# Who issues the last store, where GpSimd drains, and who clears the semaphores, at the end of a windowed attention kernel

## Chip, cores and metric

One core of a Trainium2 chip. The metric is the device time of one execution in microseconds (us), lower is better.

## The reference

```python
def reference(q, k, v):                      # each (4, 4096, 1536) float32
    W, scale = 64, 1536 ** -0.5
    # q, k, v cut into windows of 64 rows
    logits = einsum('bnwd,bnud->bnwu', q_w, k_w) * scale
    attn = softmax(logits)                   # within the window
    return einsum('bnwu,bnud->bnwd', attn, v_w)   # (4, 4096, 1536) float32
```

## The kernel before

The 16,384 rows are handled in N = 32 units of 512 rows. GpSimd issues nearly all transfers: loads of q, k, v with a cast to fp16 two units ahead, and one store of 3 MB per unit, by its software queue. SyncE starts the first loads and otherwise only watches landings. TensorE, VectorE and ScalarE compute. Only the end matters here: the last unit's store is split into two halves, so that the first can start before the last evictions are done.

```python
for u in range(1, N):                       # GpSimd's loop
    hand_over("q", u, q16, m_q, g_q)        # wait for the landing, copy, request the next load
    hand_over("k", u, k16, m_k, g_k)
    gp.wait_ge(m_q, u + 1)
    store(u - 1)                            # 3 MB, software queue, semaphore d_o[(u - 1) % 3]
    hand_over("v", u, v16, m_v, g_v)

base, o = (N - 1) * UR, outs[(N - 1) % NO]
for h, (eng, c) in enumerate(((gp, 1), (sy, 3))):   # first half GpSimd, second half SyncE
    for a in range(2):
        eng.wait_ge(n_e[a], c)              # evictions of VectorE and of ScalarE
    eng.dma_start(
        out=rows(of, base + R * P * h, R, R), in_=slots(o, R * h, R * h + R, R)
    ).then_inc(d_l[h], 16)
gp.drain()                                  # line 380
for i in range(NO):
    last = max(u for u in range(N - 1) if u % NO == i)
    sy.wait_ge(d_o[i], 16 * (last // NO + 1))
for i in range(2):
    sy.wait_ge(d_l[i], 16)                  # line 385
sy.sem_inc(done, 1)
gp.wait_ge(done, 1)
# ... lo, hi: the range of the kernel's semaphores
gp.sem_clear(range(lo, hi + 1))             # line 390
```

The softmax here doesn't subtract the row's maximum and nothing guards it: scores larger than these inputs give would overflow.

## Time and profile before

| | before |
|---|---|
| time, first three runs | 945.38 us (944.78 to 945.55) |
| the execution that was traced | 942.61 us, span 940.8 |
| 16 DMA engines | busy 90% or more in 39 of 40 slices |
| read and written | 402.65 MB, 428 GB/s over the span |
| GpSimd's drain | 928.4 to 939.6 |
| last landing | 939.04 |

For the tail, read the records of single source lines: the line, the engine (POOLq and SPq are the sequencers of GpSimd and SyncE), the operation, its duration in ns as minimum/median/maximum, and the first and last start in us of the span. A transfer's record holds its issue only; "DMA to landing" is the time from issue to the last count of its semaphore. The lines themselves stand in the prediction below.

### The profile page before, as it was taken

What the parts mean: (1) busy time and instruction counts of PE and PEld (TensorE: products, weight loads), DVE (VectorE), ACT (ScalarE), POOL (GpSimd) and SP (SyncE); (2) the same over time, 40 slices, a digit from 0 to 9 for tenths busy, and PEclk for the clock granted to TensorE, in tenths of its full rate; (3) what the DMA queues carried; (4) which work ended last, traced back from release to release, by engine and by line L of the source; (5) the groups of instructions that cost most, each with busy time, mean ns of one, the idle gap of its engine ahead of it and who ended that gap; (6) DMA issues with size and microseconds to landing.
All of it is one profiled execution on the core that took longest, in us unless ns stands there. A gap on an engine that the chain in (4) does not pass through costs nothing. (4 is left out here: it accounts for less than half of the span.)

```text
span 940.8 us, 11422 instructions
## 1 busy us (share of the span) xinstructions
PE 659.4 (70%) x4096; PEld 396.2 (42%) x3456; DVE 280.2 (30%) x453; ACT 335.6 (36%) x642; POOL 340.9 (36%) x229
## 2 busy tenths in 40 slices
PE   1888686766767767767677686776767767667673
PEld 1555244533444334454344443345534454334440
DVE  0443321333313333223332233322333223332232
ACT  1444333333333233332433333333333333343331
POOL 4344333344333442333423334333343333433221
PEclk9999978888888798877887978888888888797886
DMA  9999999999999999999999999999999999999998
GB/s 251 216 218 281 256 246 281 282 281 265 237 281 282 282 274 233 276 282 282 279 234 270 282 282 282 238 263 281 282 282 247 255 282 281 281 256 247 281 298 366
DMA packets 27084, 253.35 MB, mean 269 GB/s; under 512 B 2112, under 2 KB 2112, under 8 KB 10688
## 3 DMA queue, kind: packets, MB, share of 16 engines
q0 software_dynamic: 26352, 248.52, 100.4%
q1 hardware_dynamic: 720, 4.72, 1.3%
q14 instruction: 10, 0.08, 0.0%
q8 instruction: 2, 0.03, 0.0%
HBM read 301.99 MB, written 100.66 MB: 428 GB/s over the span
## 5 line engine op out<-in xcount | busy, mean ns | idle before, releaser
L157 PE MATMUL lt<-xq,xk 128*128 128x256 f16 x1536 | 215.5, 292 | 0.0
L145 PE MATMUL tp<-ident,k 128*128 128x128 f32 x768 | 148.5, 337 | 83.4 <-PEq L211 73.4
L294 POOL COPY v<-vl 128x3072 f32<-128x3072 f32 x31 | 85.2, 2747 | 295.9 <-DMA vl<-in_v_dram 295.9
L157 PEld LDWEIGHTS lt<-xq,xk 128*128 128x128 f16 x1536 | 159.8, 104 | 33.0
L145 PE MATMUL tp<-ident,q 128*128 128x128 f32 x768 | 110.8, 291 | 69.0 <-DVE xq L220 36.5
L145 PEld LDWEIGHTS tp<-ident,k 128*128 128x128 f32 x768 | 114.7, 175 | 103.3 <-issue 100.8
L186 PEld LDWEIGHTS <-et 128*128 128x128 f16 x384 | 35.0, 109 | 285.8 <-issue 280.3
L220 ACT COPY xk<-tp 128x512 f32<-128x512 f32 x96 | 59.3, 618 | 262.1 <-ACTq L211 262.1
L145 PEld LDWEIGHTS tp<-ident,q 128*128 128x128 f32 x768 | 90.1, 149 | 109.1 <-issue 108.4
L220 DVE COPY xk<-tp 128x512 f32<-128x512 f32 x96 | 66.5, 692 | 227.5 <-DVEq L211 227.5
L294 POOL COPY q<-ql 128x3072 f32<-128x3072 f32 x31 | 85.0, 2742 | 110.3 <-DMA ql<-in_q_dram 110.3
L294 POOL COPY k<-kl 128x3072 f32<-128x3072 f32 x31 | 85.2, 2747 | 106.9 <-DMA kl<-in_k_dram 106.9
L113 PE MATMUL o<-v,et 128*128 128x512 f16 x384 | 116.2, 448 | 0.0
L113 PE MATMUL sp<-ones,et 128*128 128x1 f16 x256 | 25.8, 170 | 116.6 <-PEq L211 114.3
L262 ACT ACTIVATE et<-lt,zeros 32x128 f16<-32x128 f32 x256 | 91.8, 359 | 39.4 <-ACTq L211 36.2
L220 ACT COPY xq<-tp 128x512 f32<-128x512 f32 x96 | 59.8, 623 | 121.3 <-ACTq L211 121.3
L249 DVE TENSOR_SCALAR out<-o,rs 128x512 f32<-128x512 f32 x128 | 91.3, 747 | 35.7 <-DVEq L211 31.7
L273 ACT ACTIVATE out<-tp,rs 128x512 f32<-128x512 f32 x64 | 44.0, 687 | 141.1 <-ACTq L211 110.9
L113 PE MATMUL tp<-v,et 128*128 128x512 f16 x256 | 92.8, 450 | 0.0
L220 DVE COPY xq<-tp 128x512 f32<-128x512 f32 x96 | 66.2, 690 | 88.7 <-DVEq L211 88.3
L239 DVE RECIPROCAL rs<-sp 128x2 f32<-128x2 f32 x64 | 10.7, 168 | 265.7 <-DVEq L211 265.2
L113 PE MATMUL lt<-v,et 128*128 128x512 f16 x128 | 58.2, 455 | 0.0
(22 smaller groups left out, 224.4 us busy)
## 6 DMA issues: line engine op xcount, KB each, us to landing
out_dram<-out POOLq DMA_DIRECT2D x31, 3072.0 KB, 61.8
ql<-in_q_dram POOLq DMA_DIRECT2D x31, 1536.0 KB, 54.9
kl<-in_k_dram POOLq DMA_DIRECT2D x31, 1536.0 KB, 54.9
vl<-in_v_dram POOLq DMA_DIRECT2D x31, 1536.0 KB, 54.9
out<-in_q_dram SPq DMA_DIRECT2D x1, 1536.0 KB, 13.4
k<-in_k_dram POOLq DMA_DIRECT2D x1, 1536.0 KB, 12.8
v<-in_v_dram POOLq DMA_DIRECT2D x1, 1536.0 KB, 19.4
out_dram<-out POOLq DMA_DIRECT2D x1, 1536.0 KB, 8.8
```

Of the source, the lines that this page charges most:

```text
L113: return nc.tensor.add_instruction(mybir.InstMatmult(name=nc.get_next_instruction_name(), engine=PE, ins=[low(rhs), low(w)], outs=[low(o)] ...
L145: ins = nc.tensor.transpose(tps[g % 2][:, r, j, :], pairs[:, c * P : (c + 1) * P], ident[:, :])
L157: ins = nc.tensor.matmul(lts[h][:, r, :, :], lhsT=halves(xk, c)[:, r, h, :, w], rhs=halves(xq, c)[:, :, h, :, w], start=(c == 0 and w == 0 ...
L186: ld = nc.tensor.ldweights(w)
L220: copy(out=dst, in_=tps[g % 2][:, :, :, :]).then_inc(f_c[g % 4], 1)
L239: ve.reciprocal(out=rs[:, n : n + R], in_=sp[:, n : n + R]).then_inc(n_d, 1)
L249: ins = ve.tensor_scalar_mul(scaled(u, n, j), bank(n, j), scalar1=rs[:, n : n + 1])
L262: ins = sc.activation(ets[h][s, :, :, s], lts[h][s, :, :, s], EXP, bias=zeros[s, 0:1], scale=scale)
L273: ins = sc.activation(scaled(u, n, j), bank(n, j), COPY, bias=0.0, scale=rs[:, n : n + 1])
L294: gp.tensor_copy(out=dst[:, :, :].bitcast(FP32), in_=landing[x][u % NL][:, :, :].bitcast(FP32)).then_inc(c_l, 1)
```

## The change

Three things at the very end of the program. Both halves are issued by SyncE. GpSimd's drain thereby stands behind the store of unit 30, the last one that GpSimd still issues, and GpSimd signals `done` when it is through. SyncE waits for `done` and the landings and clears the semaphores itself. The intent is to take GpSimd's issue, its drain and the hand-shake back to it out of the end of the chain.

```diff
-        for h, (eng, c) in enumerate(((gp, 1), (sy, 3))):
+        for h, c in enumerate((1, 3)):
             for a in range(2):
-                eng.wait_ge(n_e[a], c)
-            eng.dma_start(
+                sy.wait_ge(n_e[a], c)
+            sy.dma_start(
                 out=rows(of, base + R * P * h, R, R), in_=slots(o, R * h, R * h + R, R)
             ).then_inc(d_l[h], 16)
         gp.drain()
+        gp.sem_inc(done, 1)
+        sy.wait_ge(done, 1)
         # ... the waits for d_o and d_l on SyncE as before
-        sy.sem_inc(done, 1)
-        gp.wait_ge(done, 1)
-        gp.sem_clear(range(lo, hi + 1))
+        sy.sem_clear(range(lo, hi + 1))
```

## The prediction

> **What bounds the kernel now.** I read the page first, its slices above all, then the groups of DMA issues, the records of each source line of the tail, and last a table of stretches over the final 12 us. The two kernels differ only in the tail, so the question has two parts: what the whole run is bound by, and which event is the last one that somebody waits for.
>
> ```profile
> span 940.8 us, 11422 instructions
> ...
> DMA  9999999999999999999999999999999999999998
> ...
> q0 software_dynamic: 26352, 248.52, 100.4%
> q1 hardware_dynamic: 720, 4.72, 1.3%
> ...
> HBM read 301.99 MB, written 100.66 MB: 428 GB/s over the span
> ```
>
> The DMA row has nine tenths or more in 39 slices of 40; no compute engine is above 70%. The sum read and written, 402.65 MB, at the 428 GB/s shown is the span itself. Nothing in the change touches the 31 earlier stores or any load, so what can change is at most the last slice, 23.5 us of 940.8. A change of 2% would need 19 us, nearly all of that slice.
>
> Now the tail. Here are the issues of the last store (line 377, one half on each queue), GpSimd's drain (380), SyncE's waits for the landings (385), and GpSimd's clear (390), each with its duration in ns and its start:
>
> ```profile
> L377 POOL DMA_DIRECT2D out_dram<-out x1: 547/547/547, 928.4 to 928.4; - x1
> L377 SPq DMA_DIRECT2D out_dram<-out x1: 347/347/347, 929.5 to 929.5; - x1
> ...
> DMA to landing us min/median/max: 8.8/9.2/9.5
> ...
> L380 POOLq DRAIN  x1: 11193/11193/11193, 928.4 to 928.4; - x1
> ...
> L385 SPq EVENT_SEMAPHORE  x2: 17/22/28, 937.2 to 939.1; - x2
> ...
> L390 POOLq EVENT_SEMAPHORE_RANGE_CLEAR  x1: 353/353/353, 939.6 to 939.6; - x1
> ```
>
> The first half lands at 928.4 + 8.8 = 937.2, the second at 929.5 + 9.5 = 939.0, and SyncE passes its last wait at 939.1. It then signals `done`. But the clear on GpSimd starts only at 939.6: GpSimd's drain began at 928.4 and lasted 11.19 us, so it ended at 939.6. **The clear was held up by the drain, not by the landing.** That costs about 0.5 us at the end of the chain, and it is what the change removes. (The page's own chain of waits stops at 928.77 with VectorE, so it doesn't reach this tail; I read it from the line records.)
>
> Between them, the stretches (the six numbers in the middle are busy times of engines; DMA share and GB/s stand last):
>
> ```profile
> 929.00:930.00 1.00, 0.00 (x0) 0.00 (x0) 0.51 (x1) 0.00 (x0) 0.00 (x0) 1.00 0.99 418
> ...
> 932.00:934.00 2.00, 0.00 (x0) 0.00 (x0) 0.00 (x0) 0.00 (x0) 0.00 (x0) 0.67 1.03 434
> ...
> 936.00:937.00 1.00, 0.00 (x0) 0.00 (x0) 0.00 (x0) 0.00 (x0) 0.00 (x0) 0.50 0.96 406
> 937.00:938.00 1.00, 0.00 (x0) 0.00 (x0) 0.00 (x0) 0.00 (x0) 0.00 (x0) 0.50 0.43 184
> 938.00:939.00 1.00, 0.00 (x0) 0.00 (x0) 0.00 (x0) 0.00 (x0) 0.00 (x0) 0.50 0.12 49
> 939.00:940.00 1.00, 0.00 (x0) 0.00 (x0) 0.00 (x0) 0.00 (x0) 0.00 (x0) 0.50 0.00 0
> ```
>
> The 16 DMA engines are full from before 929 until about 937, and then drop out one by one until 938.7. When the last store is issued they still work on the store of unit 30 (issued 905.9); its 16 partial landings in the trace are spread from 929.6 to 931.7, so some DMA engines run 2.1 us behind the others. Each then has 8 + 8 packets of 12 KB of the last store, at a median of 460 ns each in the packet records: 16 x 0.46 = 7.4 us. The latest engine: 931.7 + 7.4 = 939.1, and the measured last landing is 939.04. So the latest DMA engine never ran dry, and **the landing of the last byte is set by the backlog of that engine, not by when or by whom the halves are issued.**
>
> **What the Trainium skill says.** "DMA: Bandwidth & Descriptors", section "Issuing engines are not separate DMA queues": transfers started by scalar, sync or gpsimd run on the same 16 DMA engines and interleave, and using several issuers saves only sequencer time. The trace agrees: both queues' packets take a median of 460 ns. The same page, "Latency and other measured facts", gives first bytes at about 0.6 us for the hardware path and 1 us for the software one. At the kernel's start, SyncE's first load was issued at 0.96 and its first packet ran at 1.97, so 1.0 us here; the advantage of some tenths is open. "Perfetto Trace Analysis", section "Sequencer-only Instruction (DRAIN, etc)", says that a record holds the execution and not the wait for semaphores. That agrees with the clear (353 ns, its wait for `done` not in it), and it says how to read the drain: it carries no semaphore, so its 11.19 us are its own execution, waiting for the DMAs. I found no statement on what a drain of GpSimd waits for.
>
> **The change part by part.**
> 1. First half from SyncE in place of GpSimd. The issue moves from 928.40 to about 927.9 (SyncE's condition, the third and fourth evictions of the last unit, is met at 927.88 by the semaphore records; GpSimd took 0.5 us more). The issue costs 0.35 in place of 0.55 us. Gain on the end: zero, as the latest DMA engine is busy until 931.4 with earlier work. In the traces' DMA share a dip of 0.1 for half a microsecond at 929.3 should vanish; it is on early engines, with slack of nearly 2 us.
> 2. Second half. SyncE is free of the first issue by 928.3 and still waits for VectorE's last output (its record ends at 929.51). The issue stays at 929.5. Zero.
> 3. The drain moves ahead: it now stands behind the issue of unit 30's store and the last copy of v (917.15 + 2.74 = 919.9). In the kernel before, it ended 2.3 us after the last landing on GpSimd's own queue (939.57 - 937.23). Unit 30's store lands at 931.7, or up to about 934.5 if the six or so packets still due on the latest engine alternate with packets of the first half (6 x 0.46 = 2.8 us). Plus 2.3 gives 934 to 937, ahead of 939.0: off the path. Removed from the path: 939.57 - 939.13, SyncE's last event to the end of the drain, about 0.45 us.
> 4. The clear moves to SyncE, right behind its last wait: start 939.1 in place of 939.6. I take the same 0.353 us, as it is a sequencer's work on the same range of semaphores. But before, SyncE went through its end-of-section hand-shake (four events of about 0.07 us, line 302, 939.2 to 939.4) beside GpSimd's drain and clear; now that stands behind the clear. So not all of 0.45 is gained. Working along SyncE: clear 939.10 to 939.45, first event 939.50, last gather 939.73, its no-op 939.79, its drain of the exit barrier 939.85. Before, that drain began at 940.11. Net: **-0.26 us**.
> 5. The exit barrier from there (940.11 to 940.83) is the same: 0.
>
> Sum: 0 + 0 - 0.45 + 0.19 = -0.26 us, 0.03% of the time. 945.38 - 0.26 = 945.1 us.
>
> **The rivals.**
> (a) *The drain waits for every DMA of the core, not for GpSimd's own.* Then it still ends half a microsecond behind the last landing, `done` comes at 939.6, and SyncE's clear follows: end at about the old place, 945.3 to 945.6. For it: the drain ended 0.53 us after the second half's landing too, and one record can't tell 2.3 us behind one event from 0.5 behind the other. Against: a drain at the start, with nothing outstanding, took 0.18 us, and GpSimd has nothing to do with SyncE's queue. I give this one in four.
> (b) *The hardware queue starts late.* In the kernel before, the first packet of the second half ran at 933.2, 3.7 us after its issue. If that is a delay of the queue and not its turn behind 8 packets already fetched, the first half, issued at 927.9, starts at 931.6; the latest engine could idle 0.2 us and the early ones use up their slack: +0.2 us. Against: the first-served engine needed just 8 x 0.46 = 3.7 us for the first half from 929.6, which gives the same 933.2 without any delay. One in ten.
> (c) *The stores by the hardware queue are quicker, or the late engines get relief from the software ring*, so the 1.8 us spread of the last landings shrinks. It would give up to 1 us. Against: 460 ns for packets of both queues. One in twenty.
> None of these comes near 2%.
>
> **Range and chances.** The three runs before lie within 0.8 us, more than the effect. What sets the range is therefore the run, not the mechanism: the traced execution had 942.6 where the timed ones had 945.4, so I leave about 1 us on either side, a little more below. 945.1, from 943.9 to 946.2. Faster by 2% would need 926 us, slower 964; nothing in the tail is that long, so 0.01 each, for a cause outside this reading, and 0.98 within 2%.
>
> **What would show it.** Right: GpSimd's drain starts near 920 and ends before 938; SyncE issues at about 927.9 and 929.5; the last landing stays within 0.3 us of 939.0 of that span's scale, that is 7.3 us behind the latest landing of the backlog; SyncE's clear starts within 0.15 us of the last landing and takes about 0.35 us; from the last landing to the end of the span 1.5 us in place of 1.8. Wrong: the drain ends only behind the last landing (rival a); a dip in the DMA share between 929 and 932 (rival b); packets of the hardware queue clearly under 460 ns or a smaller spread of the last landings (rival c). A time outside the range with an unchanged tail would mean that it varies between executions more than three runs show.

## The result, and the profile after

Median 943.03 us (942.75 to 943.12, 6 runs), beside 945.2 for the kernel before (943.4 to 945.7, 6 runs): ratio 0.9979, 95% interval 0.9966 to 0.9992. A ratio here is the mean time of one kernel's runs over that of the other's of the same rounds, so not quite the ratio of the medians quoted. The class "within 2%" was right; the size was not: 2.2 us were gained where 0.26 were predicted, and 943.03 lies below the range. The ratio came out as 0.9980 twice more (runs a1 and a2 below). All differences of timed runs here are far under 2%; what is read below is whether the interval leaves out 1.

The page of the changed kernel; the queues' rows show one half of the last store moved from the software queue to the hardware one, and the whole still at the same 428 GB/s:

```profile
span 941.3 us, 11422 instructions
...
q0 software_dynamic: 26208, 246.95, 100.0%
q1 hardware_dynamic: 864, 6.29, 1.7%
```

The *traced* span is longer than the traced span before (941.3 and 940.8), though the kernel is faster. So the two traces alone can't explain the gain. The records of the lines of the tail, changed kernel:

```profile
L377 SPq DMA_DIRECT2D out_dram<-out x2: 343/346/348, 927.9 to 929.1; - x2
...
DMA to landing us min/median/max: 8.4/9.7/10.9
...
L380 POOLq DRAIN  x1: 14935/14935/14935, 921.0 to 921.0; - x1
...
L387 SPq EVENT_SEMAPHORE  x2: 28/28/28, 936.4 to 940.0; - x2
...
L390 SPq EVENT_SEMAPHORE_RANGE_CLEAR  x1: 124/124/124, 940.1 to 940.1; - x1
```

The drain starts at 921.0 and ends at 921.0 + 14.9 = 935.9, over 4 us ahead of the last landing at 940.0. The clear starts less than 0.1 us behind that landing and takes 124 ns. The stretches of the tail in the changed kernel (DMA share and GB/s last):

```profile
929.00:930.00 1.00, 0.00 (x0) 0.00 (x0) 0.05 (x1) 0.00 (x0) 0.00 (x0) 1.00 1.01 430
...
932.00:934.00 2.00, 0.00 (x0) 0.00 (x0) 0.00 (x0) 0.00 (x0) 0.00 (x0) 0.50 0.95 406
...
936.00:937.00 1.00, 0.00 (x0) 0.00 (x0) 0.00 (x0) 0.00 (x0) 0.00 (x0) 0.50 0.95 406
937.00:938.00 1.00, 0.00 (x0) 0.00 (x0) 0.00 (x0) 0.00 (x0) 0.00 (x0) 0.50 0.61 258
938.00:939.00 1.00, 0.00 (x0) 0.00 (x0) 0.00 (x0) 0.00 (x0) 0.00 (x0) 0.50 0.23 98
939.00:940.00 1.00, 0.00 (x0) 0.00 (x0) 0.00 (x0) 0.00 (x0) 0.00 (x0) 0.50 0.09 37
```

The data end *later* than in the traced execution before (share 0.09 where it was 0.00). In this pair of traces nothing that moves bytes became quicker. What differs is what stands behind the last byte.

### The profile page after: what moved, and what is told of

Its sections match the earlier page's. It is cut to its first block, busy times and chain, and to the rows that moved or that the text cites. A ratio compares the mean times of both kernels' runs of the same rounds, so it can differ in the third digit from the quotient of the medians.

```text
span 941.3 us, 11422 instructions
## 1 busy us (share of the span) xinstructions
PE 655.5 (70%) x4096; PEld 395.4 (42%) x3456; DVE 279.8 (30%) x453; ACT 335.9 (36%) x642; POOL 340.4 (36%) x228
## 5 line engine op out<-in xcount | busy, mean ns | idle before, releaser
L113 PE MATMUL o<-v,et 128*128 128x512 f16 x384 | 113.6, 440 | 0.0
## 6 DMA issues: line engine op xcount, KB each, us to landing
out<-in_q_dram SPq DMA_DIRECT2D x1, 1536.0 KB, 13.9
```

Of the source, the lines that this page charges most:

```text
L113: return nc.tensor.add_instruction(mybir.InstMatmult(name=nc.get_next_instruction_name(), engine=PE, ins=[low(rhs), low(w)], outs=[low(o)] ...
```

## The experiments

All outputs are right. The theories:
- **D, the drain.** GpSimd's drain ends about 2.3 us behind the last landing on GpSimd's own queue, and in the kernel before everything that follows waits for it. How much that costs depends on how late GpSimd's half lands, which differs between executions.
- **Q, the queues.** The hardware queue brings the last landing itself forward.
- **C, the clear.** SyncE's clear and the shorter hand-shake bring it.

In the texts of expectation, "GpSimd's last landing" is the last count of the semaphore of GpSimd's last transfer; S below. L is the last landing of all. Both are read from the semaphore records of the trace. The traces together (those of drain_first_reset and mid_drain, which change the order of the work, are told below):

| kernel | S | L | drain ends | span ends | span - S | span - L |
|---|---|---|---|---|---|---|
| before (first trace) | 937.23 | 939.04 | 939.57 | 940.83 | 3.60 | 1.79 |
| b1 (before) | 938.63 | 940.45 | 940.97 | 942.23 | 3.60 | 1.78 |
| b2 (before) | 939.99 | 940.45 | 942.33 | 943.59 | 3.60 | 3.14 |
| clear_sync | 940.25 | 940.43 | 942.59 | 943.85 | 3.60 | 3.42 |
| swap | 939.55 | 939.55 | 941.89 | 943.15 | 3.60 | 3.60 |
| quarter | 938.99 | 940.36 | 941.33 | 942.59 | 3.60 | 2.23 |
| after (first trace) | 933.62 | 940.03 | 935.92 | 941.33 | | 1.30 |
| a1 (after) | 935.10 | 941.46 | 937.40 | 942.77 | | 1.31 |
| a2 (after) | 933.25 | 939.63 | 935.55 | 940.94 | | 1.31 |
| halves_sync | 933.74 | 940.14 | 936.04 | 941.49 | | 1.35 |
| halves_sync2 | 933.61 | 939.99 | 935.91 | 941.34 | | 1.35 |
| no_drain_reset | 937.98 | 939.80 | none | 941.31 | | 1.51 |

### b1 and b2: the kernel before, traced again

No edit. Each is a single execution.

> The kernel before, unchanged, for a second trace: its first traced execution took 942.6 us, its timed ones 943.4 to 945.7. Theory D (the drain): GpSimd's drain ends 2.3 us behind the last landing on GpSimd's own queue, so the end of the span is the later of two, that drain plus 1.26 us, or the last landing of all plus about 1.35 us. If this execution takes about 945, then the first half of the last store (GpSimd's) lands within 0.5 us of the second, and the drain ends over 1.5 us behind the last landing. Theory Q (the queues): the last landing itself is 2 us later than in the changed kernel (span minus last landing stays 1.8 us or less). Theory C (the clear): neither; the stretch from the last landing to the end of the span is 1.8 us as before.

> The kernel before once more, for a third trace. Theory D: end of the span 3.60 us behind the last landing of GpSimd's half, within 0.03 us, whatever the execution takes; an execution of 945 or more has that landing within 0.7 us of the last of all.

Measured: b1 944.01 us, b2 945.37 us. The tail of b2, records by line:

```profile
L377 POOL DMA_DIRECT2D out_dram<-out x1: 547/547/547, 928.7 to 928.7; - x1
L377 SPq DMA_DIRECT2D out_dram<-out x1: 347/347/347, 929.8 to 929.8; - x1
...
DMA to landing us min/median/max: 10.6/10.9/11.3
...
L380 POOLq DRAIN  x1: 13647/13647/13647, 928.7 to 928.7; - x1
...
L385 SPq EVENT_SEMAPHORE  x2: 17/22/28, 940.0 to 940.5; - x2
...
L390 POOLq EVENT_SEMAPHORE_RANGE_CLEAR  x1: 353/353/353, 942.4 to 942.4; - x1
```

SyncE has seen both landings at 940.5; the drain, begun at 928.7, lasts 13.65 us, until 942.3, and the clear starts at 942.4: 1.9 us of nothing but the drain. In the first trace the same gap was 0.5 us. b1 and b2, though from two chips, make the cleanest pair: their last landings are the same, 940.45. Their spans differ by 1.36 us, and so do their S (938.63 and 939.99). What sets the span of the kernel before is therefore not when the last byte lands, but when the last byte *of GpSimd's half* lands. b1 doesn't meet the condition of its expectation (it took 944.0, not 945, and S lies 1.8 us ahead); b2 does.

What sets L - S can be argued from the records. Call head start the time from the last landing of unit 30's store to the first packet of the second half. It was 1.4 to 1.6 us in the first trace, b1 and no_drain_reset (below), where L - S was 1.8 us, and 0.3 and 0.1 us in b2 and clear_sync (below), where L - S was 0.46 and 0.18 us. So it seems that on the DMA engine that is last the first half runs alone for the head start, and that the packets of the two queues take turns from then on. In b1 the second half was even issued 1.05 us later than in b2 (930.89 and 929.84), and the execution was the shorter one. The packed traces don't tell the DMA engine of a packet, and no run set the head start on purpose, so this isn't shown.

### clear_sync and halves_sync: each part of the change alone

clear_sync:

```diff
         gp.drain()                          # still behind GpSimd's own half
+        gp.sem_inc(done, 1)
+        sy.wait_ge(done, 1)
         # ... waits
-        sy.sem_inc(done, 1)
-        gp.wait_ge(done, 1)
-        gp.sem_clear(range(lo, hi + 1))
+        sy.sem_clear(range(lo, hi + 1))
```

> The other part alone: SyncE clears the semaphores, but GpSimd still issues the first half and drains behind it, then signals done to SyncE. Theory D: no gain, 944.8 to 945.4 us, ratio 1.000 within 0.001, because the drain still stands behind a store that lands near the end; the drain ends 2.3 us behind the first half's last landing. Theory Q: no gain. Theory C: the whole gain, 943.0.

halves_sync, run twice:

```diff
-        for h, (eng, c) in enumerate(((gp, 1), (sy, 3))):
+        for h, (eng, c) in enumerate(((sy, 1), (sy, 3))):
```

> One part of the change alone: both halves of the last store through SyncE, so that GpSimd's drain stands behind unit 30's store; SyncE still signals done to GpSimd, which clears. Theory D: nearly the whole gain, 0.15 to 0.3 per cent under the kernel before, 943.2 us (the drain ends 2.3 us behind unit 30's last landing, before the last landing of all, and the clear starts at once). Theory Q: the whole gain as well. Theory C: no gain, ratio 1.000.

> Again the one part alone, both halves through SyncE with GpSimd clearing: its first timing (ratio 0.9991, from 0.9977 to 1.0004) fell among quick executions of the kernel before and left open whether it has the whole gain. Theory D: within 0.3 us of the changed kernel beside it, ratio 0.9975 to 0.9988 to the kernel before; end of the span 1.35 us behind the last landing. If the SyncE clear adds more than its 0.05 us of the traces (1.30 in place of 1.35), this one is slower than the changed kernel by more than 0.5 us.

> The changed kernel beside it on the same chip: 943.0 to 943.4 us; end of the span 1.30 us behind the last landing.

Measured, clear_sync: 944.84 us (943.55 to 945.63), ratio 1.0004 (0.9991 to 1.0018): nothing gained, and the spread of the kernel before, 2 us, is still there (halves_sync, in the same rounds, took 943.27). Its traced execution took 945.63. Records by line, clear_sync:

```profile
L380 POOLq DRAIN  x1: 13946/13946/13946, 928.6 to 928.6; - x1
...
L387 SPq EVENT_SEMAPHORE  x2: 28/28/28, 940.3 to 940.4; - x2
...
L390 SPq EVENT_SEMAPHORE_RANGE_CLEAR  x1: 124/124/124, 942.6 to 942.6; - x1
```

SyncE stands ready at 940.4 and can clear only at 942.6, when the drain (928.6 + 13.9) lets `done` come. Theory C falls.

halves_sync: 943.27 us, ratio 0.9991 with an interval up to 1.0004. That didn't decide anything, because the kernel before happened to run quickly in those rounds (median 944.05, three of nine under 943.5). Run again beside the changed kernel, halves_sync2 gave 943.12 us (942.93 to 943.50), ratio 0.9981 (0.9968 to 0.9995), and the changed kernel (a2) 943.06 us (942.73 to 943.28), ratio 0.9980 (0.9967 to 0.9994); the kernel before had 945.28 (943.2 to 946.31). So the first part alone carries the whole measurable gain. What SyncE's clear adds is in the table: span - L of 1.30 in place of 1.35, 0.05 us, which no timing here resolves.

### no_drain_reset: the drain alone taken away

Moving both halves takes away the late drain and changes the queue at once. This run separates the two: the queues and the clear stay as they were, only the drain goes. A drain simply left out was held to be unsafe and was not run, so no run shows whether it is; GpSimd resets its DMA counts in its place, behind the wait for `done`.

```diff
-        gp.drain()
         # ... waits, done
+        gp.dma_reset(range(lo, hi + 1))
         gp.sem_clear(range(lo, hi + 1))
```

> The kernel before with its queues and its clear as they were, but without GpSimd's drain: behind the wait for done, a reset of the DMA counts (73 ns on GpSimd in the run before this) takes its place ahead of the clear. Theory D, as it now stands: the kernel before ends 3.60 us behind the last landing of GpSimd's half (three traces: 940.83 - 937.23, 942.23 - 938.63, 943.85 - 940.25), 2.34 of them the drain. Without the drain the end follows the last landing of all by about 1.45 us (1.35 in halves_sync, plus the reset), so 943.2 to 943.5 us with a spread under 0.7 us, as in the changed kernel. A theory that the gain comes from moving the first half to SyncE's queue (Q): no gain here, 944 to 945 with a spread of 2 us.

Measured: 943.09 us (942.63 to 944.00), ratio 0.9982 (0.9969 to 0.9996), beside 944.95 for the kernel before. Records by line, where the reset appears as a DRAIN of its own on line 389:

```profile
L384 SPq EVENT_SEMAPHORE  x2: 17/22/28, 938.0 to 939.8; - x2
...
L389 POOLq DRAIN  x1: 135/135/135, 939.9 to 939.9; - x1
L390 POOLq EVENT_SEMAPHORE_RANGE_CLEAR  x1: 353/353/353, 940.1 to 940.1; - x1
```

The reset takes 135 ns and the clear follows the landing by 0.3 us. The whole gain is there with the first half still on GpSimd's queue. **Theory Q falls; theory D is shown.** The time lies just under the 943.2 to 943.5 expected, and the spread was 1.4 us where I had expected under 0.7; the end of the data, L, itself varies (939.0 to 941.5 over the traces of the table).

### swap and a1

swap exchanges the two queues, so that GpSimd's half is the last one:

```diff
-        for h, (eng, c) in enumerate(((gp, 1), (sy, 3))):
+        for h, (eng, c) in enumerate(((sy, 1), (gp, 3))):
```

> The kernel before with the two queues exchanged: first half through SyncE, second through GpSimd, drain behind it. GpSimd's landing is now always the last one or near it. Theory D: always the bad end of what the kernel before shows, last landing plus 3.60 us: 945.2 to 945.8 us in every run, spread under 1 us, 0.1 to 0.2 per cent slower than before. Theory Q (a half on GpSimd's queue costs, whichever): the same as the kernel before, 944 to 945.

> The changed kernel itself, on the same chip as these others and for a second trace: 942.8 to 943.3 us, the end 1.30 us behind the last landing, the drain over 2.3 us behind unit 30's last landing and off the path.

Measured, swap: 944.93 us (944.81 to 945.54), ratio 1.0001 (0.9988 to 1.0015), beside a kernel before of 944.95 (944.35 to 945.43). The spread of 0.7 us and the end at S + 3.60 came as expected. The time did not: it lies under the 945.2 to 945.8 of theory D, and "the same as the kernel before, 944 to 945" is what theory Q had. So swap's time alone speaks for Q; it is no_drain_reset that rules Q out. That the kernel before ran near its bad end itself in all nine of its runs there (all over 944.3) would explain it, but none of the nine was read for S, so this isn't shown. a1: 943.14 us (942.24 to 944.55), ratio 0.9980 (0.9967 to 0.9994). Its end stands 1.31 us behind L; its spread is wider than I had said, and the slowest execution, the traced one, had the latest L of the table (941.46).

### quarter: less on GpSimd's queue

GpSimd keeps a store in the tail and a drain behind it, but only one row in two of the first half.

```diff
-        for h, (eng, c) in enumerate(((gp, 1), (sy, 3))):
+        first = of[base : base + R * P].rearrange("(p r) d -> p r d", r=R)
+        parts = (
+            (gp, 1, first[:, 0, :], outs[(N - 1) % NO][:, 0, :]),
+            (sy, 1, first[:, 1, :], outs[(N - 1) % NO][:, 1, :]),
+            (sy, 3, rows(of, base + R * P, R, R), slots(o, R, R + R, R)),
+        )
+        # each part with its own semaphore
```

> Graded: of the first half, GpSimd stores only one row in two (a quarter of the unit, 4 of the 8 packets of each DMA engine), SyncE the other quarter and the second half; drain behind GpSimd's part and clear as in the kernel before. Theory D: the end is the later of GpSimd's last landing plus 3.60 us and the last landing of all plus about 1.4 us. With 4 packets of 0.46 us, GpSimd's part lands between 934 and 937, over 2.2 us ahead of the last landing in most runs, so the drain is hidden: 943.0 to 943.5 us, like the changed kernel, though GpSimd still stores and drains behind it. If what costs is any store of GpSimd in the tail, or a drain that stands behind one: 944 to 945.5 like the kernel before.

Measured: 943.53 us (943.14 to 944.37), ratio 0.9984 (0.9971 to 0.9998), about where theory D had it (943.0 to 943.5): a gain, though the interval is too wide to say whether it is all of it. The traced execution was the slowest of the five:

```profile
L384 POOLq DRAIN  x1: 14295/14295/14295, 927.0 to 927.0; - x1
...
L389 SPq EVENT_SEMAPHORE  x2: 28/1738/3449, 935.6 to 940.4; - x2
...
L394 POOLq EVENT_SEMAPHORE_RANGE_CLEAR  x1: 355/355/355, 941.4 to 941.4; - x1
```

Here GpSimd's part landed at 938.99, 1.4 us ahead of L and not the 2.2 I had hoped for, so the drain still held the clear by 0.9 us (940.4 to 941.3), and the span is once more S + 3.60. My estimate of when the part lands was off; the rule held. A drain behind a late store is thus not costly as such: it costs what its end stands behind the last landing.

### drain_first_reset and mid_drain: what the drain does

drain_first_reset puts the drain ahead of GpSimd's half (with a reset of that half's count, for the same reason as above; it took 73 ns):

```diff
+        gp.drain()
         for h, (eng, c) in enumerate(((gp, 1), (sy, 3))):
             # ...
-        gp.drain()
         # ... waits, done
+        gp.dma_reset(range(d_l[0].num, d_l[0].num + 1))
         gp.sem_clear(range(lo, hi + 1))
```

> The queues as in the kernel before (first half GpSimd, second SyncE, GpSimd clears), but the drain moved ahead of the first half, and for the check a DMA reset of that half's one semaphore ahead of the clear, which costs GpSimd something of its own. The drain moved ahead will hold the issue of the first half until unit 30's store has landed plus 2.3 us, about 934, so this one isn't clean: the first half then runs last. Theory D: the end is no longer drain-bound; the time is the last landing (later by the held issue, up to 942) plus about 1.4 us, 945 or more. Theory Q: the same or slower. It tells mainly whether the drain holds GpSimd's next issue, and what the reset costs.

Measured: 945.25 us (944.32 to 945.47), ratio 1.0010 (0.9996 to 1.0024). In its trace the drain ends at 935.69, 2.30 us behind unit 30's landing at 933.39, and only then does GpSimd issue its half, at 936.3, 6 us later than SyncE issues the other. It lands at 941.63. The drain no longer stands at the end, but it has pushed the store there. So moving the drain ahead pays only when GpSimd has nothing left to issue, which is what the change sees to.

mid_drain adds a second drain to the kernel before, behind unit 16:

```diff
             hand_over("v", u, v16, m_v, g_v)
+            if u == 16:
+                gp.drain()
```

> The kernel before with one more drain of GpSimd, behind unit 16. It tells what the 2.3 us are. It will stall GpSimd until all loads and stores under way have landed, so the whole takes longer, by 10 to 50 us; only the end of its trace counts. If the last drain's 2.34 us behind GpSimd's last landing are a pass over every DMA that GpSimd has issued since its last drain (127 of them, 18 ns each; the two kernels with 126 had 2.30), it shrinks here to 55 x 18 ns = 1.0 us, and the extra drain's own is about 72 x 18 ns = 1.3 us. If they are a fixed time of a drain: 2.3 us both.

Measured: 955.72 us, one execution; the drain stopped GpSimd for 58 us and ran the DMA engines dry. The last drain ended 2.29 us behind S (952.66 and 950.37), though only 55 transfers had been issued since the drain before it; the added one ended 3.0 us behind its last landing (541.56 and 538.57) with 72. A cost per transfer, my guess, is ruled out by the first number, and one fixed time for every drain doesn't fit the second. What a drain does in these 2.3 us stays open.

## Why the prediction was wrong

Its mechanism was right, and one term of its sum was far too small. By its steps:

- **What bounds the kernel; backlog of the DMA engines.** Right. The whole runs at 428 GB/s before and after, and L shows no shift beyond its own spread, in three traces each: it was 939.04, 940.45 and 940.45 before, 940.03, 941.46 and 939.63 after. The check I had set, the last landing within 0.3 us of 939.0, was too narrow, since L differs by 1.4 us between the traces of the kernel before and by 1.8 us between those of the changed one. It also should not have been tied to "7.3 us behind the latest landing of the backlog": in the first trace after that was 940.03 - 933.62 = 6.4 us, probably because unit 30's packets now alternate with the first half's, as step 3 had allowed, and finish later. The end of all packets doesn't care.
- **Steps 1 and 2, the issues.** Right as far as it shows: 927.94 and 929.08 (929.5 had been given), and no dip in the DMA share of that trace. In a1 the packets leave a dip (to 0.63 of the engines' time near 930), with L still 6.4 us behind the backlog, so it didn't reach the last engine.
- **Step 3, the drain.** This is the step that failed, in size. I had found that the drain ends 2.3 us behind GpSimd's own last landing, and the changed kernel's drain did leave the path (935.9, inside the 934 to 937 given). But I entered the removed piece as "about 0.45 us", a difference of two times in one trace. By the prediction's own finding the term is S + 2.34 minus SyncE's last event, and it depends on how far S runs ahead of L. In the trace at hand S was 1.8 us ahead, as it was in b1, an execution of 944.0. In b2, of 945.4, which is where most timed runs are, S was 0.46 us ahead and the same term was 942.33 - 940.53 = 1.8 us; in clear_sync, of 945.6, S was 0.18 us ahead.
- **Step 4, the clear.** Wrong, with little weight: 124 ns on SyncE, not 0.353 us; from the last landing to the end it is 1.30 us, not the 1.5 given, and the part gains 0.05 us (1.35 in halves_sync) where a loss of 0.19 was entered.
- **Sum.** At the first trace's own landings the gain comes to 1.79 - 1.30 = 0.49 us, not 0.26. With b2's landings in place of the first trace's, the kernel before ends at 939.99 + 3.60 = 943.59 and the changed one would end at 940.45 + 1.30 = 941.75: 1.8 us. When S and L tie the two formulas give 3.60 - 1.30 = 2.3 us, the most they can. The measured medians differ by 2.2, 1.8 and 2.2 us in three sets of rounds. The term explains the gain, within what L and S vary; S of the timed runs isn't on record.
- **Rival (a)**, a drain that waits for every DMA, is refuted: it ended 4.1 us ahead of L after the change. **(b)** and **(c)** showed nothing in the first trace after: no dip of the share, a median of 460 ns for the packets of both queues, and a spread of the second half's 16 landings of 3 us, more than the 1.8 before.
- **The range.** The sign of the error stood in the prediction itself: "the traced execution had 942.6 where the timed ones had 945.4". I took it for noise of the run and placed it in the range. In part it was the term. The first trace was quick for two reasons: beside b2, L was 1.4 us earlier (939.04), and S was ahead of L by 1.35 us more; only the second has to do with the change. Over all executions here the kernel before has run between 942.6 and 946.3 and the changed one between 942.2 and 944.6. That fits, as the end of the one depends on the order of two queues and that of the other doesn't, but a1 alone spread over 2.3 us. A trace that is 0.3% quicker than the timed runs can show an execution in which something costly didn't happen.

No version beat the changed kernel: no_drain_reset (943.09) and halves_sync2 (943.12) equal it.

## What to carry to other kernels

If an engine drains behind its own transfer at the end of a kernel, look at which landing ends that drain, and let the last transfers be another engine's, so that the drain falls behind an earlier one. When a wait on the path depends on which of two racing events comes last, don't size it from one trace: write it as a formula of both times, and ask what it gives when they tie. And before trusting a trace for tenths of a per cent, check that its execution took what the timed ones take.

## What the Trainium skill lacked or had wrong

- "Perfetto Trace Analysis", section "Sequencer-only Instruction (DRAIN, etc)", counts only the sequencer and the semaphores as actors of a drain. No page that I found says that a drain waits for transfers. GpSimd's drain waits for those of its own queue: it lasted 11.2 to 15.0 us at the end of these kernels and ended 2.29 to 2.34 us behind the last landing on that queue (3.0 us for one in mid-kernel), and didn't wait for SyncE's (935.9 with SyncE's landing at 940.0).
- "VectorE: DVE Perf Modes", section "The DRAIN you can't avoid", gives the boilerplate drains of the runtime's preamble and postamble as about 12 ns constant on all five engines, and names no other kind but VectorE's own. The drains of this kernel's exit barrier, which may not be the same ones, took 7 to 10 ns on SyncE, ScalarE and VectorE, but 34 to 78 ns on GpSimd with nothing under way, and 183 ns at its start.
- "DMA: Bandwidth & Descriptors", section "Issuing engines are not separate DMA queues", says that starting transfers from several engines saves only sequencer time. That held for the data (a median of 460 ns a packet in both queues), but the issuer also decides what GpSimd's drain waits for, and that was worth about 2 us here (945.28 and 943.12 in halves_sync2).
- No page that I found gives the time of one instruction that clears a range of semaphores inside a kernel, or of one DMA reset of GpSimd: the same range took 353 ns on GpSimd and 124 ns on SyncE, and a reset on GpSimd 73 ns for one semaphore and 135 ns for all.
